# A seven-product block layer: another order of products for single column pairs, split operands moved to multiples of 128 bytes, and other rooms for w_pool's gates

## The chip, the cores and the metric

The kernel runs on one core of one Trainium2 chip. The metric is the device time of one execution in microseconds (us). Before the change three runs took 1486.44, 1486.37 and 1484.42 us, with a median of 1486.37 us. The profiled execution took 1487.33 us, and its span, from the first to the last instruction, is 1485.6 us. The engines are named as in the profile: PE multiplies matrices (PEld is its weight load), DVE is the vector engine, ACT the scalar engine, POOL is GpSimd, and SP issues most of the transfers between memory (DRAM) and the on-chip buffers.

## The reference

The computation is one decoder layer on x, 1024 tokens by 1024 channels, in float32:

```
proj = x @ w_in -> [q | f | i | og | pool_v | gate_a | gate_b]          (w_in: 1024 x 7168)
a    = HGRN2(q, f, i) -> per-head RMSNorm * sigmoid(og) -> @ w_a
b    = per group (causal_mean_w(pool_v) - pool_v) @ w_pool[g] * pool_scale
mix  = (sigmoid(gate_a) * a + sigmoid(gate_b) * b) @ w_out
x    = LN(alpha * x + mix)
x    = LN(alpha * x + relu(x @ w_up)^2 @ w_down)                        (w_up: 1024 x 4096)
```

HGRN2 is a recurrence per head (8 heads, 128 wide) that the kernel computes in chunks. w_pool has four groups of 256 x 256.

## The kernel before, in words

**Products.** PE multiplies float32 data in a reduced form, so every operand is split in two parts: `hi` is the rounded copy that ACT makes (a cast, L118 or L123), and `lo` is the rest, which DVE makes by subtraction (L119 or L124). One logical product is three matmuls: hi by hi, hi by lo and lo by hi. In `prod` these are lines 204, 206 and 207, each with a stationary operand of 128 x 128 (a weight part, tile `w`) and a moving operand of 128 x 512 (an activation part, tile `act`), accumulated in one PSUM bank of 128 x 512. A product of a weight block of 512 x 128 with 512 tokens has four such steps, so it is 12 matmuls.

**Pairs of columns.** The tokens and the rows of a weight matrix are halved, and two column blocks of 128 are taken together. The 2 x 2 block product then needs seven products and not eight (Winograd's form). The function `pair` (L259) makes one such pair out of four raw weight blocks b11, b12, b21, b22 of 512 x 128 and one spare tile t. Its steps so far stand in the order P1 (b11), P2 (b21), P7 (t = b22 - b12), P4 (b21 - ...), P6 (t again), P5 (b12 - b11), P3 (b22). P1, P6, P5 and P3 accumulate in turn in one bank, `ps["a"]`, and its value is taken after P1, P6, P5 and P3. P7 and P4 share the bank `ps["z"]`, P2 has `ps["c"]`. The activation operands (a11, a12, a22, s1 to s4 in `xp`) are split once per stage and stay in the 28 tiles of the pool `act`.

**Stages in order of time.** Up to about 115 us x is turned and the values i are computed, with activations stationary and weights moving (lines 470 to 472). Up to about 620 us come the pairs of the heads, the output gates, the pool values and the mixer's gates, with the recurrence between them. Then come `pool_products` for the four groups, which multiply by w_pool (lines 105 to 107 in `mm3`), and `gates` for the last columns. From about 690 us the two pairs of w_a run side by side (`a_pair`), then w_out (`mix`, again `mm3`) to about 830 us, w_up to about 1170 us (`units`; the first two pairs run side by side, all others alone), and w_down (lines 1273 to 1275) to the end, where stationary and moving operand are both `act` tiles, or `dx` tiles in the last block.

**Rings.** The raw blocks live in a ring of 6 tiles (`raw`), the split weights in a ring of 10 (`w`), the results of a pair in a ring of 2 and one of 4 (both tagged `c`), the accumulators of pairs in four PSUM banks (`pj`). A tile's next user waits until its last reader is done. `loaded_blocks` (L223) takes five raw tiles per pair in a fixed order and issues four loads on SP. In `pool_products` (L704) each of the four results of a group first gets its gate from DRAM (`gbd`), in a tile that its "room" names, and DVE's line 723 multiplies the accumulator into it; two of the four rooms are `c` tiles, the others `v` and `f`.

**Order.** No instruction order is written out by hand: a planner puts every engine's instructions in a fixed order by modelled times and by the priorities in the code, before the run. Each engine then works through its own list, and an instruction that waits holds up all that stand behind it.

**Places in the buffer.** Small constants are allocated first, then the pool `act`, both upwards from the low end; raw blocks, `w`, and the tiles `q`, `f`, `wo` lie at the high end. In the program before, every `act` tile begins 32 bytes past a multiple of 128 bytes (the first at byte 18592), as do the low `c` tiles, `dx` and the rows of x. Every `w`, `wo`, `q` and `f` tile begins on a multiple of 128 bytes (the first `w` at byte 204416). The tile `g_neg`, 32 bytes, is among the small constants.

Of the kernel before, what the change touches and what calls it, by code (L numbers as in the profile page):

```python
# [43 lines left out]
def tile_hybrid_block(  # L44
# [178 lines left out]
    def loaded_blocks(src, c1, c2, done=None):  # L223

        raw = {}
        for i in ((0, 0), (1, 0), (0, 1), "t", (1, 1)):
            raw[i] = block_tile(), None
            if i != "t":
                raw[i] = wide_block(src, i[0], (c1, c2)[i[1]], raw[i][0])
        if done is not None:  # L230
            done.append(raw[1, 1][1])
        return [raw[i][0] for i in ((0, 0), (0, 1), (1, 0), (1, 1), "t")]
# [4 lines left out]
    def w_part(src):  # L237
        return split(src, w_tile)
# [17 lines left out]
    def c_late():  # L256
        return c_tile(False)

    def pair(raw, rooms, takes, pz_tag="pj", pc_tag="pj", turned=False):  # L259


        b11, b12, b21, b22, t = raw if len(raw) == 5 else (*raw, None)
        c, ps = {}, {}

        def copied(room, ps):
            t = room()
            A.copy(t, ps)  # L267
            return t

        def added(t, ps):  # L270
            V.tensor_add(t, t, ps)  # L271
            return t

        def t3():
            c["t"] = block_tile() if t is None else t
            V.tensor_sub(c["t"], b22, b12)  # L276
            return w_part(c["t"])

        def t4():
            if turned:  # L280
                V.tensor_sub(b12, b11, b12)
                minus_sum(c["t"], b22, b12)
                minus_sum(b21, c["t"], b21)
            else:
                V.tensor_sub(b12, b12, b11)
                V.tensor_sub(c["t"], b22, b12)
                V.tensor_sub(b21, b21, c["t"])
            return w_part(b21)

        def t2():  # L290
            return w_part(c["t"])

        def t1():
            return w_part(b12)

        def p1(w):
            ps["a"] = ps_tile()
            prod(ps["a"], w, "a11", True)
            c[11] = copied(rooms[0], ps["a"])

        def p2(w):
            if pz_tag == "pj":
                ps["z"] = ps_tile()
            ps["c"] = ps_tile(pc_tag, 4 if pc_tag == "pj" else 2)
            prod(ps["c"], w, "a12", True)

        def p7(w):
            if pz_tag != "pj":
                ps["z"] = ps_tile(pz_tag, 2)
            prod(ps["z"], w, "s3", True)  # L310
            with tc.high_priority(PRIO):
                takes[0](added(c[11], ps["c"]))
                c[22] = copied(rooms[2], ps["z"])

        def p6(w):
            prod(ps["a"], w, "s2", False)
            with tc.high_priority(PRIO):
                c[21] = copied(rooms[1], ps["a"])
                takes[2](added(c[21], ps["z"]))

        def p4(w):
            prod(ps["z"], w, "a22", False)

        def p5(w):
            prod(ps["a"], w, "s1", False)
            with tc.high_priority(PRIO):
                takes[3](added(c[22], ps["a"]))

        def p3(w):
            prod(ps["a"], w, "s4", False)  # L330
            with tc.high_priority(PRIO):
                takes[1](ps["a"])

        def t0():
            return w_part(b11)

        def b_21():
            return w_part(b21)

        def b_22():  # L340
            return w_part(b22)

        return tuple(
            ((operand,), ((operand, product),))
            for operand, product in ((t0, p1), (b_21, p2), (t3, p7), (t4, p4), (t2, p6), (t1, p5), (b_22, p3))
        )

    def run(*pairs, made=(), behind=()):
# [44 lines left out]
    with tc.tile_pool(name="xr", bufs=8, side="right", reuse_waits="tile") as xr:  # L393
# [9 lines left out]
        PE.transpose(ps[:, 0:32], prm_r, ident[0:32, 0:32])  # L403
        V.tensor_copy(prm, ps[:, 0:32])
        g_col, pscale = prm[:, 16:24], prm[:, 24:32]
        g_neg = const.tile([P, 8], F32, name="g_neg")
        V.tensor_scalar_mul(g_neg, g_col, -1.0)
        lb = const.tile([P, 8], F32, name="lb")
        one_lb = const.tile([P, 8], F32, name="one_lb")
        e01 = const.tile([P, 16], F32, name="e01")  # L410
# [5 lines left out]
        V.reciprocal(lb, lb)  # L416
        V.tensor_mul(lb, lb, e01[:, 0:8])
        V.tensor_scalar(one_lb, lb, -1.0, 1.0, ALU.mult, ALU.add)
        x_rows = [xr.tile([P, CH, D], F32, name=f"x{u}", bufs=1) for u in range(2)]
        for t in range(8):  # L420
            r[t] = x_rows[t // CH][:, t % CH]
# [192 lines left out]
    with tc.tile_pool(name="tmp", bufs=1, side="right", reuse_waits="tile") as tmp:  # L614
# [88 lines left out]

        def pool_products(g):  # L704

            rooms = iter((lambda: tt("v"), c_tile, lambda: tt("f"), c_tile))
            raw = loaded(w_pool[g].rearrange("(k p) c -> p k c", p=P), lambda: block_tile((2, 2 * P)))
            pods = [[loaded(pod[2 * g + i][u], lambda: block_tile((HALF,))) for i in range(2)] for u in range(2)]
            parts = iter(("q", "f"))
# [1 line left out]
            for u in range(2):  # L711
                pl = [split(pods[u][i], row_tile) for i in range(2)]
                for i in range(2):
                    w = slice(i * P, (i + 1) * P)
                    j = 2 * g + i
                    room = next(rooms)
                    t = room() if j == KT - 1 else loaded(gbd[j][u], room)
                    ps = ps_tile()
                    mm3(ps, [(wh[:, c, w], wl[:, c, w], *pl[c]) for c in range(2)])
                    if j == KT - 1:  # L720
# [272 lines left out]
        def a_pair(p):  # L993
# [3 lines left out]
                raw[0], _ = wide_block(w_a, 0, cols[0], block_tile())  # L997
            room = mg_tile("room", 4)
            takes = [gated(2 * p + i, u, p < 2) for u in range(2) for i in range(2)]
            return pair(raw, (c_tile, room, room), takes, "hg", turned=True)  # L1000

        def unpark(*which):
            for u, j in which:
# [127 lines left out]
    with tc.tile_pool(name="up", bufs=1, side="right", reuse_waits="tile") as up:  # L1131
# [15 lines left out]
        def units(i, raw):  # L1147
# [25 lines left out]
                put(1, h12)  # L1173
                put(6, s4)

            return pair(raw, (c_tile,) * 3, (take(0), last, take(2), take(3)), "hg", "tr" if i == 2 else "pj")

        blocks = loaded_blocks(w_up, 0, P), wide_blocks(w_up, 2 * P, up_raw_tile)
        pairs = [units(i, raw) for i, raw in enumerate(blocks)]
# [212 lines left out]
```

## Time and profile before

| what | value |
|---|---|
| three runs | 1486.44, 1486.37, 1484.42 us, median 1486.37 us |
| profiled execution, its span | 1487.33 us, 1485.6 us |
| mean granted TensorE clock | 0.993 |
| busy: PE, PEld | 1463.3 us (98%), 1189.6 us (80%) |
| busy: DVE, ACT, POOL | 1132.1 us (76%), 757.5 us (51%), 80.7 us (5%) |
| data moved | 229.20 MB, mean 154 GB/s |

How to read it: a group's row gives line, engine, operation, the tiles written and read, shapes and count, then busy time and the mean duration of one in ns. Matmuls overlap, so the duration of one (some 390 ns) is not the time that it adds. What it adds is the distance from its start to the start of the next, which one reads from the list in order of time, or as a stretch of time divided by the number of matmuls in it. In the views by stretch, the number in brackets after an engine's busy time is its count of instructions; after the engines come the granted clock, the share of the DMA engines, and GB/s.

### The profile page before, as it was taken

The numbers are of one execution on the slowest core, as the hardware profiler recorded it, in microseconds if no ns is written. First come the engines' busy times: TensorE is split into PE (matmuls) and PEld (weight loads), VectorE is DVE, ScalarE is ACT, GpSimd is POOL, SyncE is SP. The second block draws the span as 40 slices with busy tenths as digits, with TensorE's granted clock in tenths as the row PEclk, the third lists the DMA queues.
The fourth block names the chain that finished last, engine by engine and source line by source line (L and its number), as shares of the span: only waits on it lengthen the run. The fifth ranks groups of instructions, "written<-read, shape, count | busy, mean of one in ns | idle before, by whom it ended". The sixth has DMA issues, their size and how long they took to land.

```text
span 1485.6 us, 20853 instructions
## 1 busy us (share of the span) xinstructions
PE 1463.3 (98%) x7377; PEld 1189.6 (80%) x7377; DVE 1132.1 (76%) x1823; ACT 757.5 (51%) x1383; POOL 80.7 (5%) x272
## 2 busy tenths in 40 slices
PE   8999999999999999899999999999999999999997
PEld 6787888888888888687788888888888888888886
DVE  4967798998998776568984598665565797878877
ACT  4445565655566566445542366555555543343435
POOL 0001010101111110000002100000000100000000
PEclk9999999999999999999999999999999999999999
DMA  7142244426435445788673134444447774535322
GB/s 255 57 134 72 79 128 142 121 93 167 111 113 137 117 117 154 244 310 270 221 238 108 47 110 166 152 144 148 135 149 262 261 284 133 176 120 183 127 71 114
DMA packets 187737, 229.20 MB, mean 154 GB/s; under 512 B 12240, under 2 KB 110576, under 8 KB 187632
## 3 DMA queue, kind: packets, MB, share of 16 engines
q1 hardware_dynamic: 181664, 213.96, 43.3%
q0 software_dynamic: 5184, 11.54, 4.1%
q10 hardware_dynamic: 784, 2.38, 0.4%
q8 instruction: 58, 0.95, 0.3%
q14 instruction: 47, 0.39, 0.1%
HBM read 150.22 MB, written 77.59 MB: 153 GB/s over the span
## 4 chain that ended last, share of the span: by engine, by line
PE 95%; DMA 2%; DVE 1%; ACT 1%; issue 0%; SPq 0%; DVEq 0%; ACTq 0%
PE ps_pj L204 17%; PE ps_pj L207 16%; PE ps_pj L206 16%; PE ps_pj L1275 4%; PE ps_pj L1273 4%; PE ps_pj L1274 4%; PE ps_pj L105 2%; PE ps_pj L106 2%; PE ps_pj L107 2%; PE ps_tr L1275 1%; PE ps_tr L1273 1%; PE ps_tr L1274 1%; PE ps_hg L207 1%; PE ps_hg L204 1%; PE ps_sc L204 1%; PE ps_sc L207 1%
## 5 line engine op out<-in xcount | busy, mean ns | idle before, releaser
L204 PE MATMUL ps_pj<-act,w 128*128 128x512 f32 x1068 | 427.9, 401 | 1.8 <-ACT w L118 1.3
L206 PE MATMUL ps_pj<-act,w 128*128 128x512 f32 x1068 | 421.4, 395 | 0.0
L207 PE MATMUL ps_pj<-act,w 128*128 128x512 f32 x1068 | 419.5, 396 | 0.0
L118 ACT CAST w<-raw 128x512 fp32r<-128x512 f32 x327 | 201.6, 620 | 311.3 <-PE ps_pj L206 188.7
L119 DVE TENSOR_TENSOR w<-raw,w 128x512 fp32r<-128x512 f32 x327 | 222.8, 688 | 102.7 <-ACT w L118 101.0
L204 PEld LDWEIGHTS ps_pj<-act,w 128*128 128x128 f32 x1068 | 200.6, 188 | 51.0 <-ACT w L118 2.9
L207 PEld LDWEIGHTS ps_pj<-act,w 128*128 128x128 f32 x1068 | 200.5, 188 | 48.9
L206 PEld LDWEIGHTS ps_pj<-act,w 128*128 128x128 f32 x1068 | 200.7, 188 | 46.0
L1235 ACT CAST act<-act 128x1024 fp32r<-128x1024 f32 x66 | 67.0, 1049 | 108.5 <-issue 35.0
L271 DVE TENSOR_TENSOR c<-c,ps_pj 128x512 f32<-128x512 f32 x95 | 65.0, 684 | 38.2 <-PE ps_pj L207 37.3
L1274 PE MATMUL ps_pj<-act,act 128*128 128x512 f32 x240 | 93.0, 389 | 0.0
L1275 PE MATMUL ps_pj<-act,act 128*128 128x512 f32 x240 | 93.0, 389 | 0.0
L1273 PE MATMUL ps_pj<-act,act 128*128 128x512 f32 x240 | 92.4, 389 | 0.0
L1236 DVE TENSOR_TENSOR act<-act,act 128x1024 fp32r<-128x1024 f32 x66 | 79.4, 1221 | 16.6 <-ACT act L1235 16.4
L267 ACT COPY c<-ps_pj 128x512 f32<-128x512 f32 x96 | 55.9, 583 | 11.3 <-PE ps_pj L207 7.9
L811 DVE RECIPROCAL tC<-tA 128x128 f32<-128x128 f32 x64 | 54.5, 909 | 0.0
L1274 PEld LDWEIGHTS ps_pj<-act,act 128*128 128x128 f32 x240 | 45.1, 188 | 9.4
L1275 PEld LDWEIGHTS ps_pj<-act,act 128*128 128x128 f32 x240 | 45.1, 188 | 9.4
L1273 PEld LDWEIGHTS ps_pj<-act,act 128*128 128x128 f32 x240 | 45.1, 188 | 9.3
L276 DVE TENSOR_TENSOR raw<-raw,raw 128x512 f32<-128x512 f32 x43 | 29.7, 690 | 23.2 <-DMA raw<-in_w_in_dram 20.4
L1144 ACT ACTIVATE c<-c 128x512 f32<-128x512 f32 x61 | 38.5, 633 | 1.5
L1143 ACT ACTIVATE c<-c 128x512 f32<-128x512 f32 x46 | 29.1, 632 | 13.9 <-DVE c L271 13.7
(408 smaller groups left out, 2665.8 us busy)
## 6 DMA issues: line engine op xcount, KB each, us to landing
h<-c SPq DMA_DIRECT2D x106, 256.0 KB, 2.8
raw<-in_w_in_dram SPq DMA_DIRECT2D x100, 256.0 KB, 3.2
act<-h SPq DMA_DIRECT2D x78, 256.0 KB, 3.0
draw<-in_w_down_dram SPq DMA_DIRECT2D x16, 1024.0 KB, 7.8
raw<-in_w_up_dram SPq DMA_DIRECT2D x56, 256.0 KB, 2.9
hf<-h SPq DMA_DIRECT2D x34, 256.0 KB, 2.9
s<-og POOLq DMA_DIRECT2D x28, 256.0 KB, 6.4
v<-v SPq DMA_DIRECT2D x16, 256.0 KB, 3.1
```

The costliest lines, as they stand in the source:

```text
L118: A.copy(hi, src)
L119: V.tensor_sub(lo, src, f(hi))
L204: PE.matmul(ps, wh[:, k], th, start=first and k == 0, stop=False, skip_group_check=True)
L206: PE.matmul(ps, wh[:, k], tl, start=False, stop=False, skip_group_check=True)
L207: PE.matmul(ps, wl[:, k], th, start=False, stop=k == CH - 1, skip_group_check=True)
L267: A.copy(t, ps)
L271: V.tensor_add(t, t, ps)
L1235: A.copy(hi, src)
L1236: V.tensor_sub(lo, src, f(hi))
L1273: PE.matmul(ps, hh[:, w], wh, start=fresh and n == 0, stop=False, skip_group_check=True)
L1274: PE.matmul(ps, hh[:, w], wl, start=False, stop=False, skip_group_check=True)
L1275: PE.matmul(ps, hl[:, w], wh, start=False, stop=n == M - 1, skip_group_check=True)
```

## The change

It has three parts. First, `pair` gets a flag `twin`. Pairs that run side by side (w_a, and the first two of w_up) keep the order of products; all others now have P1, P2, P6, P7, P5, P4, P3. In both, the block that P6 needs is built in b11 and not in t, and `loaded_blocks` takes the tile t before the tile for b12. For single pairs the sum that reads P4's bank (`takes[2]`) moves behind P4. Second, `g_neg` is no longer a tile: it is written into e01, after e01's last reader. That takes 32 bytes from ahead of the `act` tiles, so that in the built program the first of them begins at byte 18560, and every operand of a split matmul begins on a multiple of 128 bytes. Third, the four rooms of `pool_products` are tiles `v`, `q`, `f` and `og`, and no longer `c` tiles. All engines have the same number of instructions of each kind as before.

```diff
     def loaded_blocks(src, c1, c2, done=None):
 
         raw = {}
-        for i in ((0, 0), (1, 0), (0, 1), "t", (1, 1)):
+        for i in ((0, 0), (1, 0), "t", (0, 1), (1, 1)):
...
-        def t3():
+        def make_t3():
             c["t"] = block_tile() if t is None else t
             V.tensor_sub(c["t"], b22, b12)
-            return w_part(c["t"])
-
-        def t4():
+
+        def make_t2():
             if turned:
                 V.tensor_sub(b12, b11, b12)
-                minus_sum(c["t"], b22, b12)
-                minus_sum(b21, c["t"], b21)
+                minus_sum(b11, b22, b12)
             else:
                 V.tensor_sub(b12, b12, b11)
-                V.tensor_sub(c["t"], b22, b12)
-                V.tensor_sub(b21, b21, c["t"])
+                V.tensor_sub(b11, b22, b12)
+
+        def t3():
+            if twin:
+                make_t3()
+            return w_part(c["t"])
+
+        def t2():
+            if not twin:
+                make_t3()
+                make_t2()
+            return w_part(b11)
+
+        def t4():
+            if twin:
+                make_t2()
+            if turned:
+                minus_sum(b21, b11, b21)
+            else:
+                V.tensor_sub(b21, b21, b11)
             return w_part(b21)
-
-        def t2():
-            return w_part(c["t"])
...
             prod(ps["a"], w, "s2", False)
             with tc.high_priority(PRIO):
                 c[21] = copied(rooms[1], ps["a"])
-                takes[2](added(c[21], ps["z"]))
+                if twin:
+                    takes[2](added(c[21], ps["z"]))
 
         def p4(w):
             prod(ps["z"], w, "a22", False)
+            if not twin:
+                with tc.high_priority(PRIO):
+                    takes[2](added(c[21], ps["z"]))
...
+        middle = (
+            ((t3, p7), (t4, p4), (t2, p6), (t1, p5)) if twin else ((t2, p6), (t3, p7), (t1, p5), (t4, p4))
+        )
         return tuple(
-            ((operand,), ((operand, product),))
-            for operand, product in ((t0, p1), (b_21, p2), (t3, p7), (t4, p4), (t2, p6), (t1, p5), (b_22, p3))
+            ((operand,), ((operand, product),)) for operand, product in ((t0, p1), (b_21, p2), *middle, (b_22, p3))
         )
...
-        g_neg = const.tile([P, 8], F32, name="g_neg")
-        V.tensor_scalar_mul(g_neg, g_col, -1.0)
...
+        g_neg = e01[:, 0:8]
+        V.tensor_scalar_mul(g_neg, g_col, -1.0)
...
         def pool_products(g):
 
-            rooms = iter((lambda: tt("v"), c_tile, lambda: tt("f"), c_tile))
+            rooms = iter(("v", "q", "f", "og"))
...
-                    room = next(rooms)
-                    t = room() if j == KT - 1 else loaded(gbd[j][u], room)
+                    tag = next(rooms)
+                    t = tt(tag) if j == KT - 1 else loaded(gbd[j][u], lambda: tt(tag))
...
-            return pair(raw, (c_tile, room, room), takes, "hg", turned=True)
+            return pair(raw, (c_tile, room, room), takes, "hg", True, turned=True)
...
-            return pair(raw, (c_tile,) * 3, (take(0), last, take(2), take(3)), "hg", "tr" if i == 2 else "pj")
+            return pair(raw, (c_tile,) * 3, (take(0), last, take(2), take(3)), "hg", i < 2, "tr" if i == 2 else "pj")
```

More of the change, by code (lines that the diff above doesn't have):

```diff
@@ L257, in c_late, with pair @@
         return c_tile(False)
[L259 removed]
+    def pair(raw, rooms, takes, pz_tag="pj", twin=False, pc_tag="pj", turned=False):
         b11, b12, b21, b22, t = raw if len(raw) == 5 else (*raw, None)
```

## The prediction

> **What bounds the kernel now.** I read the page's busy shares first, then the chain of work that ended last, then the groups.
>
> ```profile
> span 1485.6 us, 20853 instructions
> PE 1463.3 (98%) x7377; PEld 1189.6 (80%) x7377; DVE 1132.1 (76%) x1823; ACT 757.5 (51%) x1383; POOL 80.7 (5%) x272
> ...
> PE 95%; DMA 2%; DVE 1%; ACT 1%; issue 0%; SPq 0%; DVEq 0%; ACTq 0%
> ...
> L204 PE MATMUL ps_pj<-act,w 128*128 128x512 f32 x1068 | 427.9, 401 | 1.8 <-ACT w L118 1.3
> ...
> L118 ACT CAST w<-raw 128x512 fp32r<-128x512 f32 x327 | 201.6, 620 | 311.3 <-PE ps_pj L206 188.7
> L119 DVE TENSOR_TENSOR w<-raw,w 128x512 fp32r<-128x512 f32 x327 | 222.8, 688 | 102.7 <-ACT w L118 101.0
> ...
> L1274 PE MATMUL ps_pj<-act,act 128*128 128x512 f32 x240 | 93.0, 389 | 0.0
> ...
> L276 DVE TENSOR_TENSOR raw<-raw,raw 128x512 f32<-128x512 f32 x43 | 29.7, 690 | 23.2 <-DMA raw<-in_w_in_dram 20.4
> ```
>
> PE is busy for 98% of the span and carries 95% of the last chain, so the time is a sum of matmuls. Only two things can make it shorter by much: fewer us per matmul, or the last idle 22 us. The two L rows of PE hint at the first, since the same 128x512 matmul shows 401 ns at L204 and 389 ns at L1274. Durations overlap, so the distance between starts decides. Two stretches without any wait, one wholly of lines 204 to 207 (w_up), one wholly of lines 1273 to 1275 (w_down), have these rows in the view by stretches:
>
> ```profile
> core 0: us, PE busy (x) PEld busy (x) DVE busy (x) ACT busy (x) POOL busy (x), PEclk, DMA share, GB/s
> 930.00:1130.00 200.00, 200.00 (x859) 160.67 (x858) 121.46 (x185) 107.50 (x182) 0.00 (x0) 1.00 0.48 162
> 1200.00:1400.00 200.00, 200.00 (x884) 165.68 (x883) 161.79 (x176) 78.09 (x80) 0.00 (x0) 1.00 0.49 165
> ```
>
> That is 200/859 = 232.8 ns against 200/884 = 226.2 ns, at the same clock (1.00), the same share of DMA and more DVE work in the faster one. So neither the clock nor neighbours' traffic separates them; 6.6 ns a matmul do. What does separate them shows where one line has both kinds. The list in order of time has, in w_pool's products (both operands on multiples of 128 bytes), and in w_out (stationary `act`; moving first `act`, then `w`):
>
> ```profile
> 657.35 0.39 PE L105 MATMUL ps_pj<-w,q 128*128 128x512 f32 x1
> ...
> 659.39 0.39 PE L105 MATMUL ps_pj<-w,q 128*128 128x512 f32 x1
> ...
> 782.71 0.39 PE L105 MATMUL ps_pj<-act,act 128*128 128x512 f32 x1
> ...
> 784.07 0.40 PE L105 MATMUL ps_pj<-w,act 128*128 128x512 f32 x1
> ...
> 785.23 0.40 PE L107 MATMUL ps_pj<-w,act 128*128 128x512 f32 x1
> ```
>
> From 657.35 to 659.39 are nine matmuls, 227 ns each; from 782.71 to 784.07 six with both operands `act`, 227 ns each; from 784.07 to 785.23 five with `w` and `act`, 232 ns each. Nothing else changes at 784.07 but the tile. Before the change `act` begins 32 bytes past a multiple of 128, `w` and `q` on one. Fast are 32 with 32 and 0 with 0; slow is 0 with 32, whichever operand streams. The change makes all of them 0 with 0.
>
> **The change part by part: the alignment.** The slow kind is all of lines 204 to 207 and 470 to 472, and in w_out the matmuls that read `w` or `wo`. Counts of one of the three lines each:
>
> ```profile
> 0.00:1486.00 1486.00, 492.07 (x1232) 231.31 (x1232) 0.99 0.48 154
> 0.00:1486.00 1486.00, 43.28 (x112) 21.73 (x112) 0.99 0.48 154
> 100.00:620.00 520.00, 248.61 (x616) 115.40 (x615) 1.00 0.45 124
> ```
>
> The rows are of line 204 (x1232), line 470 (x112), and line 204 between 100 and 620 us (x616). Lines 204 to 207: 3 x 1232 x 6.6 ns = 24.4 us. Lines 470 to 472: 3 x 112 x 6.6 = 2.2 us, but that stage waits for x and its first weights to arrive, so between 0 and 2.2; I take half, 1.1. In w_out six matmuls in eight steps with moving `w` or `wo`, twelve tiles of tokens by halves: 3 x 48 = 144 matmuls, 0.9 us. The sum is 26.4 us. One instruction more or less in each stretch moves the 6.6 ns by 0.5, so 24 to 29 us. DVE and ACT gain nothing: at L119 all operands are already on 128, and the mean is the 688 ns it shows for every other 128x512 subtraction of this page (690 at L276). `g_neg` itself is one instruction that moves back a few places on DVE, 171 ns, far from any end:
>
> ```profile
> L407 DVE TENSOR_SCALAR g_neg<-prm x1: 171/171/171, 8.4 to 8.4; 128x8 f32<-128x8 f32 x1
> ```
>
> **The order of products.** No engine gains or loses an instruction: 7 casts, 7 subtractions, 4 block sums a pair as before, and the four loads of a pair stand in the same order on SP; POOL's list is not touched. What moves is distance. Before, P6, P5 and P3 followed each other in one bank, each waiting for the value to be taken; now P7 and P4 stand between. That gain is bounded by what PE waits for today, in the view of waits:
>
> ```profile
> PE ps_pj L105 <- DVE c L723: 4.7, 1, 4.7
> PE ps_pj L204 <- ACT w L118: 1.3, 3, 0.5
> PE ps_pj L204 <- ACT room L267: 0.5, 1, 0.5
> DVE raw L276 <- DMA raw<-in_w_in_dram: 20.4, 12, 4.6
> ```
>
> The planner has hidden nearly all of it behind other pairs: 1.8 us in all for lines 204 to 207. Against that, the third operand now needs three block sums instead of one, 2 x 0.69 = 1.4 us more behind the last block's arrival. DVE waits for that arrival 12 times, so the loss is at most 12 x 1.4 = 17 us; behind the waiting sum are queued DVE's subtractions for the next products. The cover is the ring of ten `w` tiles, up to four products of 2.8 us (12 x 233 ns) ahead, and PE never waited for L276's chain between 100 and 600 us. The slots that the next pair's b12 and b22 take come free at the same steps as before (the fourth and the fifth). I take 0, ends +17 and -1.8.
>
> **w_pool's rooms.** The one long stall of PE is there:
>
> ```profile
> 616.65 8.30 DMA raw<-in_w_in_dram
> ...
> 621.99 0.39 PE L107 MATMUL ps_pj<-w,f 128*128 128x512 f32 x1
> 625.07 0.69 DVE L276 TENSOR_TENSOR raw<-raw,raw 128x512 f32<-128x512 f32 x1 [4.63 <-DMA raw<-in_w_in_dram]
> 626.28 0.75 DVE L723 SCALAR_TENSOR_TENSOR c<-ps_pj,prm,c 128x512 f32<-128x512 f32 x1
> 627.08 0.79 PE L105 MATMUL ps_pj<-w,q 128*128 128x512 f32 x1 [4.71 <-DVE c L723]
> ...
> 629.38 0.63 PE L107 MATMUL ps_pj<-w,f 128*128 128x512 f32 x1
> ...
> 625.00:650.00 25.00, 22.44 (x86) 17.57 (x87) 15.12 (x23) 9.13 (x16) 0.00 (x0) 0.86 0.87 318
> ```
>
> DVE waits 4.63 us for a block of the next gates; behind it stand the L723 that empty w_pool's banks, so PE stands still for 4.7 us and then starts at half clock: 627.08 to 629.38 are five matmuls of 0.46 us. The mean clock of 0.86 over these 25 us is some 7 us at half, half of it in the gap; the rest costs some 12 matmuls 0.2 us each, 2.4 us. With the short waits after it that is about 8 us. In the changed program all four L723 of w_pool's first group stand ahead of that sum, since `q` and `og` need no `c` tile. PE then has the remaining product (6 matmuls, 1.4 us) and the next P1 (2.8 us) to do during the wait. But the last two of those blocks now stand on SP behind two w_a loads of 512 KB: 1 MB at 318 GB/s, 3.3 us. Ends: 8 us gained, 3.3 us lost; I take a gain of 2.5, near the middle.
>
> **What is late next.** With PE faster by 2.8%, DVE comes nearer:
>
> ```profile
> 225.00:450.00 225.00, 225.00 (x1425) 183.76 (x1424) 209.62 (x423) 131.70 (x303) 25.82 (x109) 1.00 0.43 123
> 675.00:775.00 100.00, 98.66 (x423) 78.62 (x421) 87.88 (x142) 53.95 (x97) 0.00 (x0) 1.00 0.70 230
> ```
>
> In the first stretch, by the count above, PE saves 12.2/520 a us, 5.3 us; DVE's 209.6 us still fit into 219.7, at 95%. In the second 87.9 fit into 97.7. So DVE does not become the bound, but waits will grow; I take 1 us, between 0 and the whole saving of those stages (12.2 us between 100 and 620, and 2.3 in the second stretch: 14.5).
>
> **The sum.** 26.4 + 0 + 2.5 - 1 = 27.9 us less than the profiled execution's 1487.33 us (its span and 1.7 us around it) is 1459.4. That execution lies 0.96 us above the median of the three runs; from the median, 1486.37 - 27.9 = 1458.5 us.
>
> **The rivals.** First, the offset is not what separates fast from slow. In every slow row one operand lies at the low end of the buffer (`act`) and the other at the high end; in every fast row both lie on one side. If the side decides, nothing becomes faster, since nothing changes sides. Against it: two operands on one side should get in each other's way more, not less. The time would be 1486.4 - 2.5 + 1 for the rest, about 1485 us, between 1477 and 1494. Two statements of the Trainium skill speak for this rival. In "SBUF — State Buffer", section Specifications (TRN2), the lines of the buffer have 16 bytes, and 32 bytes past a multiple of 128 is the start of such a line, so that no more lines are read than before. In "TensorE: Matmul & The Clock Gate", section Back-to-back issue gap, the distance of two matmuls is N/2.4 + 2.5 ns with no term for where operands lie, 216 ns for 512 columns; by that the sum would be without its 26.4 us. This case's trace does not agree: it has 226 and 233 ns for one shape at one clock.
>
> Second, the matmuls become faster and the supply does not follow: DVE's and ACT's chains, at 93% of DVE in the first stretch above, end last wherever DVE is that full. Then the 14.5 us of those stages are lost again: 1458.5 + 13.5 = 1472 us. For it speaks that DVE's list is in order; against it that L119 waits 101 us for ACT, and ACT 188.7 us for PE (rows above), that is, the suppliers today wait for PE.
>
> Third, slower: the third operand of single pairs comes too late. There are 38 single pairs (44 less four of w_a and two of w_up). Its three sums and the split take 3 x 0.69 + 0.62 + 0.69 = 3.4 us from the last block's landing, against 2.0 us before. If PE has used up its lead, every pair waits. At 0.73 us a pair the gain of 27.9 us is gone; at the full 1.4 us the time is 1458.5 + 53 = 1512 us. Against it: w_up's 930 to 1130 us have no PE wait at all, with DVE at 61%.
>
> **How the numbers follow.** Forecast (alignment works, supply follows): 0.83, with its own range from 1451 (all 8 us of the stall gone too) to 1467 (17 us of late third operands half paid). Offset without effect: 0.08, 1485 us. Supply does not follow: 0.05, 1472 us. Third operand late: 0.04, 1512 us. The time 1458.5 is the forecast's. The range 1450 to 1474 takes in the forecast and the second rival, and leaves out the other two. A change below 0.2%, 3 us, is about what a measurement here can't tell from none. Faster by more than that: 0.83 + 0.05 + 0.04 of the first rival = 0.92. The same: 0.03. Slower: 0.04 + 0.01 = 0.05.
>
> **What the changed profile would show.** Right: the stretch of w_up has about 884 matmuls in 200 us, like w_down, the mean at line 204 falls from 401 towards 389 ns, and w_down and the durations on DVE and ACT stay. The wait of 4.7 us on L723 is gone or short, with a clock near 1.00 around it. Wrong: starts still 233 ns apart in w_up (first rival); 227 ns apart, but with new PE waits on ACT at lines 118 or 119 between 225 and 450 us or around 700 us (second); waits before P6 in each single pair, with DVE's first block sum behind a DMA (third). What would make the prediction wrong beyond these is a new stall near w_pool, where loads are dense and the planner's list is new.

## The result, and the profile after

Four runs of the changed kernel took 1470.92 to 1475.04 us, median 1472.24 us; four runs of the kernel before (the three above and one more) had a median of 1486.40 us. The ratio is 0.991, with a 95% interval of 0.9893 to 0.9928. So 14.2 us are gained where 27.9 were forecast. The profiled execution took 1472.13 us, its span is 1470.4 us. From its page:

```profile
span 1470.4 us, 20890 instructions
...
PE 1438.7 (98%) x7377; PEld 1188.8 (81%) x7377; DVE 1127.7 (77%) x1823; ACT 760.6 (52%) x1383; POOL 82.2 (6%) x272
...
PE 92%; DVE 3%; DMA 3%; issue 1%; ACT 1%; SPq 0%; DVEq 0%; ACTq 0%
...
L204 PE MATMUL ps_pj<-act,w 128*128 128x512 f32 x1068 | 422.3, 396 | 8.3 <-DVE q L742 5.8
L207 PE MATMUL ps_pj<-act,w 128*128 128x512 f32 x1068 | 414.0, 391 | 1.7 <-DVE w L119 1.7
...
L276 DVE TENSOR_TENSOR raw<-raw,raw 128x512 f32<-128x512 f32 x43 | 29.5, 689 | 30.1 <-DMA raw<-in_w_in_dram 27.3
```

PE's busy time fell by 24.6 us (1463.3 to 1438.7), but the span by only 15.2: PE's idle time rose from 22.3 to 31.7 us, and DVE and DMA now hold 6% of the last chain instead of 3%. The matmuls became as fast as forecast; new waits took back 9.4 us of it. The first half of that sentence is in the view by stretches (columns as in the prediction), w_up first, then w_down, then the heads:

```profile
930.00:1130.00 200.00, 200.00 (x884) 165.62 (x883) 125.21 (x192) 112.54 (x191) 0.00 (x0) 1.00 0.51 174
1200.00:1400.00 200.00, 200.00 (x884) 165.62 (x883) 159.78 (x174) 76.54 (x79) 0.00 (x0) 1.00 0.45 147
225.00:450.00 225.00, 223.94 (x1483) 186.19 (x1482) 205.98 (x421) 135.14 (x299) 26.93 (x104) 1.00 0.46 126
```

w_up has 884 matmuls in 200 us, 226.2 ns each, just like w_down, whose own count did not move. The means at lines 204 and 207 fell only to 396 and 391 ns and not to 389; a mean over all of a line's matmuls also holds those that start after a wait, so the stretch is the better measure. The second half is in the view of waits:

```profile
PE ps_pj L204 <- DVE q L742: 5.8, 1, 5.8
PE ps_hg L204 <- ACT room L267: 2.9, 1, 2.9
```

The long stall in w_pool is still there (5.8 us, formerly 4.7). The one of 2.9 us is new, and longer than any other wait of the profile before, whose next longest, 2.2 us, is for x at the start.

Where they lie is told by a table. All programs compared here have the same 5856 split matmuls, stage after stage, so the time between the n-th and the m-th can be compared stage by stage, from the starts in the list in order of time. The second column is what the prediction's 6.6 ns make of the slow matmuls counted in that stage; the others are measured changes against the profile before, in us. E1, E5 and E2 are experiments told below.

| stage (us, before) | worked out | changed kernel | E1: alignment alone | E5: both operands at 32 | E2: order and rooms alone |
|---|---|---|---|---|---|
| 0 to 100, stage one | -2.2 | -2.7 | -2.3 | -2.4 | -1.1 |
| 100 to 322, heads | -5.4 | -5.0 | -4.6 | -3.4 | -0.5 |
| 322 to 561, heads | -5.6 | -2.7 | -3.3 | -0.4 | +0.5 |
| 561 to 616, gates | -1.2 | -0.9 | -1.0 | -1.0 | -0.9 |
| 616 to 689, w_pool | -1.3 | -0.4 | -0.2 | -1.6 | -0.2 |
| 689 to 733, w_a's start | -1.2 | +3.1 | +0.2 | +2.3 | +5.0 |
| 733 to 863, w_a, w_out | -2.0 | -2.1 | -2.1 | -2.2 | 0.0 |
| 863 to 917, w_up's start | -1.5 | +2.7 | -1.3 | -1.3 | +3.6 |
| 917 to 1173, w_up | -7.1 | -7.2 | -7.2 | -7.2 | 0.0 |
| from 1173, w_down | -0.1 | -0.1 | +1.0 | 0.0 | +0.7 |

Stage one, w_out and w_up paid out the worked-out gain in full. In the changed kernel the heads paid some 8 of 11 us, w_pool next to nothing, and the starts of w_a and w_up each turned a gain of over 1 us into a loss of about 3. w_pool and the two starts are explained below; the heads stay open. These profiles are single executions, and the four runs of one kernel lie 2 to 5.6 us apart (E1's profile is of the fastest of its four, E5's of the slowest), so I read no difference below some 2 us out of one of them. What w_pool withheld, 0.9 us, is below that; its stall rests on the view of waits.

In w_pool, the chain of waits has this (start, length, what):

```profile
611.04 0.43 DVE v L742
611.47 7.17 DMA raw<-in_w_in_dram
618.72 0.70 DVE raw L276
...
620.05 0.76 DVE q L742
620.94 0.77 PE ps_pj L204
621.71 0.43 PE ps_pj L206
```

The four multiplications that empty the banks of w_pool's first group are done by 608.1 us, well ahead of the sum at L276 that waits for the block. But PE has meanwhile gone on to the second group, and of its four (v, q, f, og) only the first stands ahead of the sum. The second, L742 into `q`, comes at 620.05, behind a wait of 7 us, and PE waits for its bank. From 621.71 on, matmuls of 0.43 us follow. The queue of SP shows what the block stands behind:

```profile
604.83 2.71 SPq L215 DMA_DIRECT2D raw<-in_w_a_dram  x2
...
609.36 0.74 SPq L215 DMA_DIRECT2D raw<-in_w_in_dram  x1
610.19 1.18 SPq L743 DMA_DIRECT2D pb<-q  x1
611.47 0.44 SPq L215 DMA_DIRECT2D raw<-in_w_in_dram  x1
```

Two loads of w_a take 2.7 us to issue and the store `pb<-q` 1.2 us; the last block goes out at 611.47 and needs 7.2 us to land.

At w_a's start the longest wait, the 2.9 us above, ends with a copy on ACT. From the list in order of time of ACT and PE:

```profile
687.42 1.14 ACT L123 CAST act<-c 128x512 fp32r<-128x512 f32 x2 [5.04 <-DMA c<-o]
...
688.99 0.58 ACT L267 COPY room<-ps_hg 128x512 f32<-128x512 f32 x1
...
689.62 0.50 PE L204 MATMUL ps_hg<-act,w 128*128 128x512 f32 x1 [2.88 <-ACT room L267]
```

The copy stands in ACT's list behind casts that wait 5 us for `c<-o`, loads of the heads' outputs. SP's list shows what has changed about these: before, all of them are issued ahead of the gates `ga`; in the changed kernel `ga` loads stand ahead of the last four. SP's list before, and then in the changed kernel:

```profile
689.80 1.04 SPq L587 DMA_DIRECT2D c<-o  x2
...
695.58 4.11 SPq L587 DMA_DIRECT2D ga<-ga  x8
```

```profile
677.78 1.74 SPq L606 DMA_DIRECT2D ga<-ga  x3
679.64 0.36 SPq L606 DMA_DIRECT2D c<-o  x1
...
680.83 0.32 SPq L606 DMA_DIRECT2D c<-o  x1
```

The last four `c<-o` need 6.3 us in the middle from issue to landing, where they needed 3.5 before. E2, E8 and E11, the other programs with both the new order of single pairs and the new rooms, have `ga` ahead of `c<-o` as well, and the same wait for this copy (1.7 to 2.1 us). The place of `ga` need not be all: E9, where it stands behind, has the wait with 1.4 us. The shorter waits that follow, up to 704 us, end a chain of loads of `ga` and w_a:

```profile
686.77 5.37 DMA ga<-ga
692.16 5.64 DMA raw<-in_w_a_dram
...
703.95 0.50 PE ps_pj L207
```

At w_up's start it is DVE nearly without a gap (of the 10.3 us from 866.28 to 876.55 all but some 1.2 are DVE):

```profile
866.28 0.50 ACT act L123
...
873.49 2.08 DVE c L191 x4
...
875.82 0.69 DVE w L119
876.55 0.50 PE ps_pj L207
```

Neither loss needs fast matmuls: E2 in the table has both losses with the old, slow ones.

### The profile page after: what moved, and what is told of

Its sections match the earlier page's. It is cut to its first block, busy times and chain, and to the rows that moved or that the text cites. A ratio compares the mean times of both kernels' runs of the same rounds, so it can differ in the third digit from the quotient of the medians.

```text
span 1470.4 us, 20890 instructions
## 1 busy us (share of the span) xinstructions
PE 1438.7 (98%) x7377; PEld 1188.8 (81%) x7377; DVE 1127.7 (77%) x1823; ACT 760.6 (52%) x1383; POOL 82.2 (6%) x272
## 4 chain that ended last, share of the span: by engine, by line
PE 92%; DVE 3%; DMA 3%; issue 1%; ACT 1%; SPq 0%; DVEq 0%; ACTq 0%
PE ps_pj L204 16%; PE ps_pj L207 16%; PE ps_pj L206 15%; PE ps_pj L1292 4%; PE ps_pj L1294 4%; PE ps_pj L1293 4%; PE ps_pj L107 2%; PE ps_pj L105 2%; PE ps_pj L106 2%; PE ps_tr L1292 1%; PE ps_tr L1294 1%; PE ps_tr L1293 1%; PE ps_sc L207 1%; PE ps_sc L206 1%; PE ps_sc L204 1%; PE ps_hg L204 1%
## 5 line engine op out<-in xcount | busy, mean ns | idle before, releaser
L204 PE MATMUL ps_pj<-act,w 128*128 128x512 f32 x1068 | 422.3, 396 | 8.3 <-DVE q L742 5.8
L207 PE MATMUL ps_pj<-act,w 128*128 128x512 f32 x1068 | 414.0, 391 | 1.7 <-DVE w L119 1.7
L206 PE MATMUL ps_pj<-act,w 128*128 128x512 f32 x1068 | 415.3, 390 | 0.0
L276 DVE TENSOR_TENSOR raw<-raw,raw 128x512 f32<-128x512 f32 x43 | 29.5, 689 | 30.1 <-DMA raw<-in_w_in_dram 27.3
```

Source lines behind the costliest of these rows:

```text
L204: PE.matmul(ps, wh[:, k], th, start=first and k == 0, stop=False, skip_group_check=True)
L206: PE.matmul(ps, wh[:, k], tl, start=False, stop=False, skip_group_check=True)
L207: PE.matmul(ps, wl[:, k], th, start=False, stop=k == CH - 1, skip_group_check=True)
```

## The experiments

**E1, alignment alone.** The kernel before, with one edit. Every engine's list is the one of before, except that one small DVE instruction moves.

```diff
-        g_neg = const.tile([P, 8], F32, name="g_neg")
-        V.tensor_scalar_mul(g_neg, g_col, -1.0)
...
+        g_neg = e01[:, 0:8]
+        V.tensor_scalar_mul(g_neg, g_col, -1.0)
```

> The kernel before with the second part of the change alone: g_neg written into e01, so that every act tile begins on a multiple of 128 bytes; every engine's list is that of the kernel before, but for the place of one small instruction. Theory A (the new orders of products and rooms brought new stalls and ate half of the gain): starts 226.7 ns apart as in the changed kernel, none of its new stalls, 1459 to 1463 us. Theory B (PE got faster and the supply of operands does not follow, whatever the order): 1468 to 1474 us, with new PE waits on ACT and DVE in the same places as in the changed kernel.

Measured: 1468.45 us (1465.99 to 1469.30), ratio 0.9876 [0.9857, 0.9894]. The 930 to 1130 us have 884 matmuls, and PE's busy time in its profile is 1437.8 us, 25.5 us less than before, where 26.4 were worked out:

```profile
PE 1437.8 (98%) x7377; PEld 1188.8 (81%) x7377; DVE 1128.4 (77%) x1823; ACT 757.1 (52%) x1383; POOL 81.8 (6%) x272
```

```profile
930.00:1130.00 200.00, 200.00 (x884) 165.60 (x883) 122.36 (x187) 109.99 (x185) 0.00 (x0) 1.00 0.51 171
```

So one edit of 32 bytes, with nothing else, gives 18 us by the medians, more than the whole change. But it gives 18 and not 26: the spacing is right, and part of the gain ends in waits (PE's idle time in the profile, a run 2.5 us faster than the median, rose from 22.3 to 26.5 us). The time is theory B's.

**E2, order and rooms without the alignment.** The changed kernel with `g_neg` as a tile again, so the edit above taken back.

> The changed kernel with g_neg as a tile of its own again, so with the new order of products and the new rooms, and act tiles 32 bytes past a multiple of 128. Starts 233 ns apart again by both theories. Theory A: slower than the kernel before by the new stalls, 1493 to 1500 us. Theory B: 1484 to 1489 us, since at the old pace of PE the supply had sufficed.

Measured: 1493.98 us (1492.80 to 1496.48), ratio 1.0053 [1.0034, 1.0072], slower by 7.3 us than the runs of before beside it. Its w_up is as slow as before:

```profile
930.00:1130.00 200.00, 200.00 (x859) 160.64 (x858) 119.51 (x183) 108.26 (x184) 0.00 (x0) 1.00 0.45 151
```

The two parts that I had put at 0 and -2.5 cost 7.3 us by themselves. In the profile the starts of w_a (+5.0) and w_up (+3.6) make more than the whole of it. Here the time is theory A's, so neither theory holds alone.

**E3 and E4, the alignment with one of the two.** E3 is the kernel before with E1's edit and the new rooms; E4 is the changed kernel with the old rooms:

```diff
-            rooms = iter(("v", "q", "f", "og"))
+            rooms = iter((lambda: tt("v"), c_tile, lambda: tt("f"), c_tile))
...
-                    tag = next(rooms)
-                    t = tt(tag) if j == KT - 1 else loaded(gbd[j][u], lambda: tt(tag))
+                    room = next(rooms)
+                    t = room() if j == KT - 1 else loaded(gbd[j][u], room)
```

> The kernel before with the alignment and the new rooms of w_pool, and the old order of products. Theory A with the loss in the order of products: 1456 to 1461 us, a little below the alignment alone. Theory A with the loss in the rooms: 1466 to 1472 us. Theory B: 1468 to 1474 us.

> The kernel before with the alignment and the new order of products, and the old rooms of w_pool. Theory A with the loss in the order of products: 1468 to 1475 us. Theory A with the loss in the rooms: 1459 to 1463 us. Theory B: 1468 to 1474 us.

Measured: E3 1464.73 us (1463.66 to 1469.08), ratio 0.9859 [0.9837, 0.9881]; E4 1468.34 us (1466.63 to 1468.89), ratio 0.9876 [0.9858, 0.9893]. The rooms added to the alignment take 3.7 us off it, at the edge of what these runs can tell; the order of products changes nothing; both together (the changed kernel) add 3.8. The parts do not add up; the planner makes a new list for every program. E3's time lies between theory A's two cases; E4's agrees with the loss in the order and with theory B. E3 is faster than the changed kernel beyond both intervals.

**E5 and E6, which offset counts.** E5 is the kernel before with a padding at the high end of the buffer made smaller, so that `w`, `wo`, `q` and `f` begin 32 bytes past a multiple of 128, as `act` does. E6 is the kernel before with one more unused constant of 32 bytes, so that `act` begins 64 past it and `w` at 0. Neither changes an engine's list.

```diff
-    G.memset(pad.tile([P, 24], F32, name="pad_top"), 0.0)
+    G.memset(pad.tile([P, 16], F32, name="pad_top"), 0.0)
```

```diff
+        const.tile([P, 8], F32, name="gap")
```

> The kernel before with the pad at the high end cut from 96 to 64 bytes, so that w, wo, q and f begin 32 bytes past a multiple of 128, as act does; no engine's list changes. If it is the agreement of the two operands' offsets that counts: starts about 227 ns apart in w_up, 1459 to 1463 us, as with both on 128. If each operand must begin on a multiple of 64 or 128: 233 ns and 1485 to 1488 us, or slower. If the side of the buffer decides: 233 ns and 1486 us.

> The kernel before with one more unused constant of 32 bytes ahead of act, so that act begins 64 bytes past a multiple of 128 and w on one; no engine's list changes. If offsets need to agree by 64 bytes: starts 227 ns apart and 1459 to 1463 us. If they need to agree by 128 bytes: 233 ns and 1486 us.

Measured: E5 1467.72 us (1465.83 to 1470.02), ratio 0.9872 [0.9857, 0.9887]; E6 1474.94 us (1473.46 to 1476.33), ratio 0.9923 [0.9907, 0.994]. The w_up stretch, E5 and then E6:

```profile
930.00:1130.00 200.00, 200.00 (x884) 165.64 (x883) 122.43 (x186) 111.27 (x189) 0.00 (x0) 1.00 0.51 173
```

```profile
930.00:1130.00 200.00, 200.00 (x875) 164.10 (x874) 122.83 (x187) 110.52 (x188) 0.00 (x0) 1.00 0.50 170
```

With no operand on 128 bytes, E5 has the full speed: what counts is that the two operands agree in their place. Over how many bytes they have to agree is open: in all fast pairs of these programs the places are equal within 512 bytes too (the first `act` and `w` tiles, at 18560 and 204416, leave 128, and E5's leave 160), so 128, 256 and 512 are not told apart. E5's operands are on opposite sides of the buffer, so the side does not matter. At 64 and 0 (E6) it is 200/875 = 228.6 ns, between 226.2 and 232.8.

**E7 and E8, which part of the new order.** E7 is the changed kernel with the old sequence of products for all pairs; E8 lets only the pairs that run side by side build P6's block in t again.

```diff
     def pair(raw, rooms, takes, pz_tag="pj", twin=False, pc_tag="pj", turned=False):
+        twin = True
```

```diff
+        def at():
+            return c["t"] if twin else b11
...
-                minus_sum(b11, b22, b12)
+                minus_sum(at(), b22, b12)
...
-                V.tensor_sub(b11, b22, b12)
+                V.tensor_sub(at(), b22, b12)
...
-            return w_part(b11)
+            return w_part(at())
...
-                minus_sum(b21, b11, b21)
+                minus_sum(b21, at(), b21)
...
-                V.tensor_sub(b21, b21, b11)
+                V.tensor_sub(b21, b21, at())
```

> The changed kernel with the old order of products for all pairs; the block for P6 still built in b11, the spare tile still earlier in the ring, alignment and rooms as changed. If the new order of single pairs is what costs the changed kernel its 7 us against alignment with rooms: 1463 to 1467 us, without the waits of 3.3, 1.9 and 1.4 us near 686, 700 and 875 us. If building the block in b11 (and the ring) costs it: 1470 to 1474 us, with these waits.

> The changed kernel with the pairs that run side by side (w_a and the first two of w_up) building the block for P6 in the spare tile again, as before; single pairs in the new order. If the new order of single pairs costs: 1470 to 1474 us. If the pairs side by side with b11 cost: 1463 to 1467 us, and the waits near 686, 700 and 875 us gone, since all of them lie where pairs run side by side.

Measured: E7 1469.08 us (1465.84 to 1470.25), ratio 0.988 [0.9861, 0.9899]; E8 1472.45 us (1470.88 to 1473.36), ratio 0.9905 [0.9889, 0.9921]. E8 is the changed kernel's time: the place of P6's block in the twin pairs is not it. E7 has no loss at w_a's start (+0.1 us against before, where the changed kernel has +3.1), but it keeps the one at w_up's start (+3.1). E7's time lies between its two expectations. So the sequence of the single pairs takes part in the first loss and not in the second. It does not make the first alone: E4, with the new sequence and the old rooms, has -0.8 us at w_a's start and +0.5 at w_up's. The second goes with the rooms: E3, E9 and E10, with new rooms and the old order, have +1.3 to +1.4 us at w_up's start, E1 and E12, with old rooms, -1.3.

**E9 and E10, what is queued on SP near w_pool.** Both start from E3. E9 issues the stores of w_pool's results on POOL's queue; E10 holds w_a's first loads until the last block of the last single pair before them is issued.

```diff
-                    nc.sync.dma_start(out=pbd[j][u], in_=t)
+                    nc.gpsimd.dma_start(out=pbd[j][u], in_=t)
```

```diff
+        gate_loads = []
...
-                loaded_blocks(w_in, 5 * D + j * P, 6 * D + j * P), rooms,
+                loaded_blocks(w_in, 5 * D + j * P, 6 * D + j * P, gate_loads if j == 6 else None), rooms,
...
-        two = [a_pair(p) for p in range(2)]
+        with tc.issue_after(gate_loads[0].ins):
+            two = [a_pair(p) for p in range(2)]
```

> Alignment and new rooms with the old order (1464.7 us), and the stores of w_pool's results issued on POOL and not on SP, so that no store that waits for DVE stands ahead of the last weight blocks. If that place in SP's list makes the stall of 5 to 6 us on w_pool's banks: the wait falls under 2.5 us and the time to 1459 to 1462 us. If the transfers are late because all the queues are full there: the stall stays, 1463 to 1467 us.

> Alignment and new rooms with the old order (1464.7 us), and w_a's first loads, three of 512 KB, held behind the last weight block of the gates that stall. If those loads make that block late: the stall of 5 to 6 us on w_pool's banks falls by 2 to 3.5 us, and the time to 1461 to 1463 us. If the stores ahead on SP make it late: the stall stays over 4 us, 1464 to 1467 us.

Measured: E9 1471.42 us (1469.46 to 1472.76), ratio 0.9898 [0.9881, 0.9915]; E10 1465.48 us (1464.41 to 1466.56), ratio 0.9857 [0.9838, 0.9875]. E9 lies above both expectations: in it the stall is longer, in its chain of waits because of the same kind of block:

```profile
607.81 11.81 DMA raw<-in_w_in_dram
```

In E10 it falls into two of 2.6 and 2.3 us, the second because another transfer is now last:

```profile
616.40 5.37 DMA q<-gb
...
622.31 0.50 PE ps_pj L204
```

E10's time is E3's. A reason is suggested by the 24 us about the stall, first before (whose stall ends 6 us later), then in the changed kernel, then E10:

```profile
610.00:634.00 24.00, 18.81 (x73) 14.48 (x73) 15.36 (x24) 7.58 (x13) 2.62 (x3) 0.86 0.99 307
```

```profile
604.00:628.00 24.00, 18.16 (x69) 14.48 (x69) 13.44 (x22) 7.42 (x14) 0.80 (x1) 0.86 1.07 356
```

```profile
604.00:628.00 24.00, 19.92 (x80) 15.67 (x79) 14.49 (x24) 7.58 (x14) 2.63 (x3) 0.93 1.07 334
```

The DMA engines are full there in all three (a share of 0.99 before, 1.07 in both later kernels). In these runs, whatever was put first, something else came last.

**E11 and E12, the same hold elsewhere.** E11 is the changed kernel with E10's hold, E12 is E1 with it.

> The changed kernel, with one edit: w_a's first loads are held on SP until the last weight block of the mixer's last single pair (gates(6)) has been issued. Theory A (in the changed kernel both the stall in w_pool and the waits at w_a's start are made by the order of transfers on SP): the 6.2 us between two starts near 615 us falls to 3 us or less, the 3.3 us near 686 us falls too, and the time comes to 1465 to 1469 us. Rival B (the time that the hold saves is lost again behind it, as it was when the hold was put on the kernel with alignment and rooms alone, 1464.7 to 1465.5 us): the stall is shorter, but the time stays at 1471 to 1474 us.

> The kernel before with g_neg written into e01 (alignment alone), and the same hold of w_a's first loads; old order, old rooms. Theory A: the 5.8 us gap near 610 us falls to 3 us or less and the 1468.4 us of alignment alone become 1464 to 1467 us. Rival B: the time stays at 1467 to 1470 us.

Measured: E11 1469.61 us (1467.69 to 1473.25), ratio 0.9884 [0.9868, 0.99]; E12 1466.24 us (1464.03 to 1469.15), ratio 0.9859 [0.9842, 0.9876]. E11's time lies between the two expectations, and theory A's mechanism is borne out by half: between 590 and 625 us there are now two distances between starts of 2.7 and 3.2 us (6.2 before the hold), the second with `q<-gb` last again, but w_a's start keeps its gaps (2.1, 1.9 and 1.4 us). E12 has A's time, but its stall is 5.4 us between starts and E1's is 5.8, so the time proves nothing for A. With the runs' spread of 2 to 5 us, E1, E3, E10 and E12 are not told apart from each other.

**E13 and E14, DVE relieved in the heads.** Both compute something else: the recurrence uses the decay where its inverse belongs. E13 is the kernel before with this edit, E14 has E1's edit as well.

```diff
-                V.reciprocal(r[:, w], fd[:, w])
+                V.tensor_copy(r[:, w], fd[:, w])
```

> The kernel before with line 811 of the recurrence, 64 reciprocals of 128x128 on DVE, replaced by copies: the recurrence then computes with the decay instead of its inverse, and DVE has some 40 to 50 us less to do between 225 and 600 us. It is the base for the next run, which adds the alignment and has the same lists of instructions but for one small one. Both theories expect 1478 to 1490 us, since PE hardly waits there today.

> The run above with g_neg written into e01, nothing else. Theory A (alignment alone gave 18 and not 26 us because DVE in its order could not follow in the heads): with DVE relieved there the two runs differ by 23 to 27 us, and the windows 225 to 450 us have no PE wait on DVE. Rival B (what is lost lies at the dense loads of w_pool and at w_a's start, which this leaves as they are): the two differ by 17 to 20 us.

Measured: E13 1506.72 us (1505.15 to 1510.94), ratio 1.0133 [1.0116, 1.0151]; E14 1489.59 us (1485.86 to 1491.13), ratio 1.0009 [0.9998, 1.002]. The alignment is worth 17.1 us here, as rival B had it, though DVE is now busy for 84% of 225 to 450 us and not 93% (E13):

```profile
225.00:450.00 225.00, 220.67 (x1395) 179.50 (x1393) 189.84 (x422) 129.39 (x292) 46.66 (x114) 1.00 0.45 123
```

But the base was not what either theory expected. With 44 us less to do on DVE (64 operations of 215 and not 898 ns) it became 19 us slower, and PE, never idle between 225 and 450 us before, now waits there for 4.3 us. A possible reason shows on POOL, whose small steps of the recurrence became slower. The first row is of before, the second of E13:

```profile
L813 POOL COPY T<-tA 128x32 f32<-128x32 f32 x16 | 5.9, 368 | 242.0 <-DVE tA L805 242.0
```

```profile
L813 POOL COPY T<-tA 128x32 f32<-128x32 f32 x16 | 15.4, 965 | 206.1 <-DVE tA L805 206.1
```

In the Trainium skill, "GPSIMD Engine Reference", section Specifications, POOL's way into the buffer is shared with DVE, and contends when DVE runs in a two-port mode or reads two inputs from the buffer. The rows would fit that, but no run here separates it from the new list that the planner made. So this pair says that DVE's share of busy time alone is not what withholds the gain. It does not say which wait of the heads does.

## Why the prediction was right and wrong

**The alignment, -26.4 us: the mechanism and the size of one matmul were right.** 232.8 ns became 226.2 ns, the figure taken from w_down, and the stages without waits gave what was counted: w_up -7.2 us for 7.1 worked out, w_a and w_out -2.1 for 2.0. The spacing that the Trainium skill's page "TensorE: Matmul & The Clock Gate", section Back-to-back issue gap, gives, without a term for where operands lie, would have left all this out; E1 and E5 show that in this kernel the place counts. Only the rule was put too narrowly: 32 with 32 is as fast as 0 with 0, as the prediction had read from the rows before, so the multiple of 128 bytes that the change aims at is not needed. The nine w_pool matmuls shown as fast were a fast stretch: the nine just ahead of them, from 655.27 to 657.35 us, lie 231 ns apart with their operands in the same places. What shows the rule is E1 and E5, not those rows.

**"What is late next", +1 us: mis-sized.** This term should have been about 8. E1, which has the alignment and nothing else, gained 18.2 us by the medians (1486.70 to 1468.45) where 26.4 - 1 were forecast, so 7 us are missing by the medians (4 in E1's profile). The prediction took 1 out of a range of 0 to 14.5, on the ground that DVE's work still fits the shorter stage at 95%. E1's column puts 3 us of the loss into the heads and some 1 us each into w_a's start, both named by the prediction, and into w_pool, which it left out of this term; the smaller ones are below what one execution can tell. A share below 100% over a stage did not mean that the saving comes through: in w_pool a transfer's landing ends last, and there the faster PE waited longer (5.4 us in E1, 4.7 before). The second rival, 1472 us, is therefore half true: the saving does not all come through, but that full DVE and ACT lists withhold it is not shown, and E14 speaks against it for the heads. That it names the changed kernel's time is chance: half of the changed kernel's loss comes from elsewhere.

**The order of products, 0, and the rooms, -2.5: the step that failed.** Without the alignment the two cost 7.3 us (E2); with it 3.8 (E1 to the changed kernel). The prediction followed the edited pairs by themselves and looked for a price where the edit is (the third operand's sums, a bank in w_pool). That the loads of one pair keep their order on SP is so, but loads of other kinds changed places. The price is paid elsewhere: the planner's new list puts `ga` ahead of the heads' outputs at w_a's start, and at w_up's start a chain of DVE's work ends last. The prediction bounded the order by +17, from the third operand; that rival (1512 us) was not seen: DVE's wait for blocks at L276 rose from 20.4 to 27.3 us, but w_up's single pairs run without a PE wait. It priced nothing around w_a and w_up, though the new order of every engine's instructions was fixed before the run and could be read there as well as in w_pool.

**w_pool.** The prediction had the first group's four multiplications ahead of the sum that waits for a block, and they are. What it did not see is who is late next: the second group's second multiplication stands behind the same sum, and the wait of 4.7 us became 5.8. It also had w_a's loads ahead of the last two blocks, priced at up to 3.3 us of loss, and the outcome lies on that side: no gain, a wait 1.1 us longer, and a clock of 0.86 in the 24 us about it where the prediction looked for 1.00. Neither rooms (E3), another queue (E9) nor a hold (E10) removes the wait. That the stretch is bound by transfers fits this (DMA share 0.99 to 1.07), but no run had less to move there, so it is argued and not shown.

**The sum.** 27.9 forecast, 14.2 measured; of the missing 13.7 us some 7 are gains of the alignment that end in waits, and some 6 are the new lists (3.8 lost where 2.5 were to be gained). The measured time lies inside the range, near its upper end, because the range took in the second rival. The first rival, that the side of the buffer decides, is refuted by E5. The argument against it, that operands on one side hinder each other more, is not borne out either: w_down (one side) and E5's w_up (two sides) both have 226.2 ns. Still open is which wait withholds the gain in the heads (3 to 7 us by E1 and E5), and what in the planner's order moves `ga`.

**Faster than both.** The kernel before with the alignment and the new rooms, and the old order of products (E3), takes 1464.73 us; with the hold (E10) 1465.48 us.

## What to carry to other kernels

Give a matmul's two operands the same place within 128 bytes (here they also had it within 512) and check it by the spacing of starts in a stretch without waits, not by the duration of one. Count such a saving in full only for stretches in which PE waits for nothing; where transfers or a dependent chain already end last somewhere, count nothing there until a run shows it. When a planner orders the work, an edit has its price wherever the new list differs, so build the parts of a change separately: here 32 bytes gave 18 us, and the parts that looked like fine tuning took 4 back.

## What the runs showed of the hardware

**Offsets have more than two speeds, and the operand that streams matters.** With `act` at 64 and `w` at 0 (E6), lines 204 to 207 run at 228.6 ns, but the first stage's lines, where `act` is stationary and `w` streams, stay at the slow speed. From E6's list in order of time, the first stage (six distances, 233 ns each; its lines are numbered one higher than before), then w_up (seven, 230 ns each, 228.6 over the whole stretch):

```profile
68.79 0.39 PE L473 MATMUL ps_pj<-w,act 128*128 128x512 f32 x1
...
70.19 0.39 PE L473 MATMUL ps_pj<-w,act 128*128 128x512 f32 x1
```

```profile
999.61 0.39 PE L204 MATMUL ps_sc<-act,w 128*128 128x512 f32 x1
...
1001.22 0.39 PE L206 MATMUL ps_pj<-act,w 128*128 128x512 f32 x1
```

Why is not settled by these runs.

**Half clock after gaps of very different length.** After 6.2 us between two starts (changed kernel, 614.7) PE runs at half clock, 0.43 us a matmul, until 626.4. E11 has half clock after much less, in its list in order of time:

```profile
593.69 0.39 PE L933 MATMUL ps_hg<-st,tA 128*128 128x128 f32 x2
596.46 0.50 PE L204 MATMUL ps_pj<-act,w 128*128 128x512 f32 x1 [2.38 <-ACT c L267]
...
597.34 0.63 PE L204 MATMUL ps_pj<-act,w 128*128 128x512 f32 x1
...
599.90 0.63 PE L204 MATMUL ps_pj<-act,w 128*128 128x512 f32 x1
```

After 2.65 us without a start (593.8 to 596.46), PE runs on at full clock for 0.9 us and then, from 597.34 to 599.90, six matmuls of 0.43 us each. In the changed kernel a distance of 3.27 us at 686.3 is followed by none of these, at a clock of 1.00:

```profile
684.00:692.00 8.00, 5.12 (x23) 3.91 (x22) 5.42 (x9) 4.18 (x8) 0.00 (x0) 1.00 1.05 392
```

The Trainium skill, "TensorE: Matmul & The Clock Gate", section "What's actually happening", has the clock fall after at least one idle window of about 3.4 us that runs freely. That the length of a gap alone does not decide agrees with these runs. That a whole window of 3.4 us has to be idle does not: in E11 2.65 us were enough (a granted clock of 0.52 from 597 to 600.5), and in E10 a distance of 2.3 us, behind which matmuls stand 0.43 us apart from 622.96 to 625.95; E10's first distance, of 2.6 us, has none behind it.

**A kernel with less work on DVE was slower.** E13 took 44 us off DVE and lost 19 us, with POOL's copies at 965 and not 368 ns. Whether DVE, POOL or the planner's new list did it is not shown.
